# Matmuls grouped by their width, and the first layer's attention in pairs with its division on GpSimd

## The chip, the core and the metric

The kernel runs on one core of a Trainium2 chip. The metric is the device time of one execution in microseconds. A core has engines that run side by side: TensorE (PE: matmuls; PEld: the loads of their stationary operand), VectorE (DVE), ScalarE (ACT), GpSimd (POOL) and SyncE (SP), which here issues nearly all DMAs. An engine runs its own instructions in order; semaphores join the engines.

## What is computed

Two transformer layers on 256 tokens of width 1024 in float32, each followed by a squared-ReLU MLP of width 4096, then a final RMSNorm. The first (even) layer has 8 heads of neighbourhood attention (NA) beside 8 heads of latent attention (MLA); the second (odd) layer has 16 heads of dilated windows in three groups.

```python
def even_mixer(xn, w_in, rpb, ...):
    hcat = xn @ w_in
    out_a = neighbourhood_attention(q, k, v, rpb)          # softmax(q k / 8 + bias) v, 8 heads of 64
    out_b = dense_attention(q, k, v, (64 + 32) ** -0.5)    # 8 heads, q and k of 96, v of 64
    return jnp.concatenate([out_a, out_b], axis=-1) @ w_o

def sq_relu_mlp(xn, w1, w2):
    return jnp.square(jax.nn.relu(xn @ w1)) @ w2

for layer in range(2):
    x = x + (even_mixer if layer == 0 else odd_mixer)(rms_norm(x, norm_mix[layer]), ...)
    x = x + sq_relu_mlp(rms_norm(x, norm_mlp[layer]), mlp_w1[layer], mlp_w2[layer])
return rms_norm(x, norm_final)
```

## The kernel before

**Number format.** A float32 operand is split into a high and a low part (`split`, L200: a CAST on ACT makes `whi`, a subtraction on DVE makes `wlo`), and a product is the sum of three matmuls, high by high, high by low and low by high. `mm3` (L204) issues them as three matmuls of one width. Where the moving operand is the layer's input, its two parts lie side by side (`pair_tile`, L87: 256 tokens high, 256 low), and two matmuls do: a **wide** one of 512 columns, `whi` by both parts, and a **narrow** one of 256 columns, `wlo` by the high part. Both have a 128x128 stationary operand.

**Where wide and narrow matmuls are.** `up` in `mlp` (L390 and L391): 32 steps (16 in each MLP), each with two PSUM banks (f = 0, 1) and 8 k, so 16 wide and 16 narrow in turn. Between two `up` steps stand the 24 matmuls of a `down` step, all 512 wide (`mm3`). In the odd layer `gemm` of `qk_steps` (L905, L906): 24 weights, two banks each, 8 k, in two halves of 4 k; between the halves and the banks stands attention work (`weave`). In the first `up` step of an MLP the wide matmul of k needs the parts of the input that `join` (L298) has just made: DVE adds the layer's output to x (L301), ACT makes the high part (L241), DVE the low part (L242), two k at a time. `hand_over` runs the last steps of the output projection (`out_last`, on PE) and these joins.

**The first layer's attention.** 16 items, 8 of NA and 8 of MLA; an item is a pair of heads (hp) by a half of the tokens (t). An item has three steps. `scores` (L730): on PE 6 matmuls with 64 rows (NA, `two_heads`, L214) or with 96 (MLA); then on DVE two reductions (L748 or L751), on ACT two exponentials (L753), on DVE a reciprocal (L754), on ACT two scalings by it (L756). `turn_probs` (L759): four transposes on PE (L763) and a copy out. `mix` (L767): eight matmuls of 64 columns (L777; float32, so a trace has two records for each of four pairs), and a `split` of the 128x128 result. `attention()` lists the steps item by item; the loop at L818 puts them between the steps of `main` (projections, then the output projection), each of which carries a cost number, in proportion to the cost that has gone by.

**Second layer's attention** has the same three steps; its `mix` (L995) puts two halves of the tokens into two banks, with one `split` each. **The end** (`finish`, L489 to L509): the last 128 tokens are scaled by their norm in two halves, one on DVE and one on ACT, each stored by its engine's own DMA (SP's for DVE).

PE, ACT, DVE and POOL instructions are ordered by a scheduler that keeps dependencies and follows priorities (`tc.high_priority`); weights come through four `raw` buffers, loaded four ahead and split two ahead (L192).

Of the kernel before, what the change touches and what calls it, by code (L numbers as in the profile page):

```python
# [16 lines left out]
F32 = mybir.dt.float32  # L17
# [23 lines left out]
NORM_PRIO = 300  # L41

# [26 lines left out]
def trunk(ctx, tc, a, out):  # L69
# [304 lines left out]
    def mlp(mp, xT, s, invert, tail, make_down, beside=lambda j: None):  # L374
# [4 lines left out]
        def up(j):  # L379
            w = weight()  # L380


            pu = [bank("w") for _ in range(2)]

            ranges = [range(4), range(4, 6), range(6, 8)] if j == 0 else [range(8)]
            for ks in ranges:
                for f in range(2):
                    for k in ks:
                        c = slice(k * 256 + f * P, k * 256 + f * P + P)
                        nc.tensor.matmul(two(pu[f]), w[0][:, c], xT[2][:, k], start=k == 0, stop=False)  # L390
                        nc.tensor.matmul(pu[f][:, 0:T], w[1][:, c], xT[0][:, k, :], start=False, stop=k == KT - 1)  # L391
# [48 lines left out]
    def finish(mp, xT, s):  # L440
# [49 lines left out]
        xg = [scratch([512], "xg") for _ in range(2)]  # L490
        residual(1, HALF[1], accs[3])
        for i, (c0, c1) in enumerate(((0, 512), (512, 768), (768, D))):
# [11 lines left out]
            nc.vector.tensor_tensor(xg[c0 // 512][:, c0 % 512:c0 % 512 + c1 - c0], v, g[:, c0:c1], op=ALU.mult)  # L504
        r = rsqrt(ss[:, 3:4], "x")
        nc.vector.tensor_scalar(xg[0], xg[0], r, None, ALU.mult)
        nc.sync.dma_start(out[P:T, HALF[0]], xg[0])
        nc.scalar.activation(xg[1], xg[1], AF.Copy, scale=r)
        nc.scalar.dma_start(out[P:T, HALF[1]], xg[1])  # L509


    def even(ep):
# [208 lines left out]
        items = [(0, t, hp) for hp in range(4) for t in range(NT)] + [(1, t, hp) for hp in range(4) for t in range(NT)]  # L721
# [8 lines left out]
        def scores(n):  # L730
# [24 lines left out]
            for j in range(2):  # L755
                nc.scalar.activation(pp[:, j], pp[:, j], AF.Copy, scale=rz[:, j:j + 1])  # L756
# [10 lines left out]
        def mix(n):  # L767
            kind, t, hp = items[n]
            pts = turned.pop(n)
# [3 lines left out]
            pvo = bank("acc" if n < 6 else "w")  # L773
            for kk in range(NT):
                for j in range(2):
                    h = 2 * hp + j
                    nc.tensor.matmul(pvo[64 * j:64 * j + 64, 0:P], v[:, kk, h * 64:(h + 1) * 64], pts[:, 2 * j + kk, :],  # L777
                                     start=kk == 0, stop=kk == NT - 1)
            split(*(z[:, hp, tok(t)] for z in mixed[kind]), pvo[:, 0:P])

        def attention():

            out = []
            for n in range(len(items) + 2):
# [3 lines left out]
                if n == 0:  # L788
                    out += [lambda: None] * 2
# [373 lines left out]
```

## Time and profile before

| what | value |
|---|---|
| median of 3 runs (lowest to highest) | 747.52 us (747.17 to 747.56) |
| the profiled execution | 746.66 us |
| its span, first to last instruction | 744.8 us |
| TensorE clock granted, mean | 0.999 |
| PE busy | 737.3 us, 99% of the span |
| DVE, ACT, POOL busy | 539.9, 473.6, 8.3 us |
| first layer, up to the first wide matmul of its MLP | 0 to 113.4 us |

A busy PE says little by itself: a matmul's shown duration covers its way through the array, and neighbours overlap (a wide one shows 397 ns, and the next starts about 230 ns later). So the pace is read from starts: first and last start of a run of like matmuls, over their number. "Who waited for whom" and the chain of work that ended last tell whether PE stood still.

### The profile page before, as it was taken

How to read it: one execution, taken by the hardware profiler on the slowest of the kernel's cores; microseconds unless marked ns; L12 is line 12 of the kernel's file. 1: busy time of each engine (PE TensorE's matmuls, PEld its weight loads, DVE VectorE, ACT ScalarE, POOL GpSimd, SP SyncE). 2: the span in 40 equal slices, each digit the busy share in tenths (PEclk: the TensorE clock that was granted, in tenths of full speed). 3: DMA queues.
4: the chain of work that ended last, by engine and by line, in shares of the span. 5: the costliest groups of instructions: out<-in, count | busy, mean ns of one | idle time of the engine just before them, and what ended most of it. 6: DMA issues, size and time to landing. Idle time of an engine off the chain costs nothing.

```text
span 744.8 us, 12006 instructions
## 1 busy us (share of the span) xinstructions
PE 737.3 (99%) x4539; PEld 634.8 (85%) x4539; DVE 539.9 (72%) x1109; ACT 473.6 (64%) x1027; POOL 8.3 (1%) x20
## 2 busy tenths in 40 slices
PE   9999999999999999999999999999999999999996
PEld 7998998888888887888888888888898888888885
DVE  6778858766666667689968886899558765665664
ACT  7788866554554556468877768687856544554541
POOL 0100000000000001000000000000000000000000
PEclk9999999999999999999999999999999999999999
DMA  9772334565555554645654555455545556555501
GB/s 292 309 272 97 118 113 166 175 222 178 187 201 178 191 196 152 234 159 172 213 209 144 191 175 180 136 194 169 194 148 181 194 191 205 184 177 191 193 13 56
DMA packets 24585, 133.17 MB, mean 179 GB/s; under 512 B 3664, under 2 KB 4688, under 8 KB 10192
## 3 DMA queue, kind: packets, MB, share of 16 engines
q1 hardware_dynamic: 24384, 132.15, 51.4%
q8 instruction: 35, 0.57, 0.3%
q10 hardware_dynamic: 144, 0.26, 0.1%
q14 instruction: 22, 0.18, 0.1%
HBM read 127.16 MB, written 1.05 MB: 172 GB/s over the span
## 4 chain that ended last, share of the span: by engine, by line
PE 97%; issue 1%; ACT 1%; DVE 0%; POOLq 0%; POOL 0%
PE w L390 16%; PE acc L205 13%; PE acc L207 13%; PE acc L206 13%; PE acc L905 12%; PE w L391 8%; PE acc L906 6%; PE acc L553 3%; PE w L214 1%; PE w L991 1%; PE w L205 1%; PE w L207 1%; PE w L763 1%; PE w L206 1%; PE w L971 1%
## 5 line engine op out<-in xcount | busy, mean ns | idle before, releaser
L202 DVE TENSOR_TENSOR wlo<-raw,whi 128x512 fp32r<-128x512 f32 (+2 forms) x471 | 304.6, 680 | 128.7 <-ACT whi L201 128.0
L201 ACT CAST whi<-raw 128x512 fp32r<-128x512 f32 (+2 forms) x471 | 262.4, 615 | 173.4 <-PE w L390 62.4
L390 PE MATMUL w<-pair,whi 128*128 128x512 f32 x512 | 182.2, 397 | 0.0
L391 PE MATMUL w<-pair,wlo 128*128 128x256 f32 x512 | 144.2, 282 | 0.0
L905 PE MATMUL acc<-pair,whi 128*128 128x512 f32 x384 | 139.2, 403 | 0.0
L390 PEld LDWEIGHTS w<-pair,whi 128*128 128x128 f32 x512 | 96.5, 189 | 23.1
L906 PE MATMUL acc<-pair,wlo 128*128 128x256 f32 x384 | 108.1, 282 | 0.0
L205 PE MATMUL acc<-whi,hh 128*128 128x512 f32 x250 | 98.2, 393 | 0.0
L207 PE MATMUL acc<-whi,hl 128*128 128x512 f32 x250 | 97.9, 391 | 0.0
L206 PE MATMUL acc<-wlo,hh 128*128 128x512 f32 x250 | 97.8, 391 | 0.0
L391 PEld LDWEIGHTS w<-pair,wlo 128*128 128x128 f32 x512 | 96.1, 188 | 0.9
L905 PEld LDWEIGHTS acc<-pair,whi 128*128 128x128 f32 x384 | 72.4, 189 | 16.8 <-issue 0.2
L906 PEld LDWEIGHTS acc<-pair,wlo 128*128 128x128 f32 x384 | 72.3, 188 | 0.0
L207 PEld LDWEIGHTS acc<-whi,hl 128*128 128x128 f32 x250 | 47.0, 188 | 9.9
L205 PEld LDWEIGHTS acc<-whi,hh 128*128 128x128 f32 x250 | 47.0, 188 | 9.8
L206 PEld LDWEIGHTS acc<-wlo,hh 128*128 128x128 f32 x250 | 47.0, 188 | 8.9
L394 ACT COPY side<-w 128x256 f32<-128x256 f32 x64 | 23.6, 369 | 22.1 <-PE w L391 22.1
L205 PE MATMUL acc<-whi,pair 128*128 128x512 f32 x80 | 32.4, 405 | 0.0
L207 PE MATMUL acc<-whi,pair 128*128 128x512 f32 x80 | 31.5, 394 | 0.0
L206 PE MATMUL acc<-wlo,pair 128*128 128x512 f32 x80 | 31.2, 390 | 0.0
L395 DVE TENSOR_TENSOR u<-w,side 128x256 f32<-128x256 f32 x64 | 26.9, 420 | 3.7 <-ACT side L394 3.0
L201 ACT CAST hh<-hsq 128x512 fp32r<-128x512 f32 x32 | 19.9, 622 | 10.1 <-DVE hsq L397 10.1
(221 smaller groups left out, 1102.9 us busy)
## 6 DMA issues: line engine op xcount, KB each, us to landing
raw<-in_w SPq DMA_DIRECT2D x64, 1024.0 KB, 4.9
raw<-in_w_oqk SPq DMA_DIRECT2D x24, 1024.0 KB, 5.2
raw<-in_w_ov SPq DMA_DIRECT2D x12, 1024.0 KB, 4.9
raw<-in_w_qk SPq DMA_DIRECT2D x4, 1024.0 KB, 8.9
raw<-in_w_oe SPq DMA_DIRECT2D x4, 1024.0 KB, 5.0
sw<-qk SPq DMA_DIRECT2D x64, 64.0 KB, 2.1
raw<-in_w_oo SPq DMA_DIRECT2D x4, 1024.0 KB, 5.0
bias<-in_rpb SPq DMA_DIRECT2D x8, 256.0 KB, 3.9
```

Of the source, the lines that this page charges most:

```text
L201: a = nc.scalar.copy(hi, src).ins
L202: return a, (eng or nc.vector).tensor_tensor(lo, src, hi.bitcast(F32), op=ALU.subtract).ins
L205: nc.tensor.matmul(o, sh, mh, start=first, stop=False)
L206: nc.tensor.matmul(o, sh, ml, start=False, stop=False)
L207: nc.tensor.matmul(o, sl, mh, start=False, stop=last)
L390: nc.tensor.matmul(two(pu[f]), w[0][:, c], xT[2][:, k], start=k == 0, stop=False)
L391: nc.tensor.matmul(pu[f][:, 0:T], w[1][:, c], xT[0][:, k, :], start=False, stop=k == KT - 1)
L394: nc.scalar.copy(side[:, f], pu[f][:, T:2 * T])
L395: nc.vector.tensor_tensor(u[:, f], pu[f][:, 0:T], side[:, f], op=ALU.add)
L553: nc.tensor.matmul(o[:, 0:n], xs[i], (w[1], w[1], w[2])[i], start=(k, i) == (0, 0), stop=(k, i) == (KT - 1, 2))
L905: nc.tensor.matmul(two(pq), wh[:, ws], xp[:, k], start=k == 0, stop=False)
L906: nc.tensor.matmul(pq[:, 0:T], wl[:, ws], xh[:, k, :], start=False, stop=k == KT - 1)
```

## The change

- `up` and the odd layer's `qk_steps` issue a bank's wide matmuls in a run and then the narrow ones in a run. In `up` all 16 wide ones of both banks come first; in `qk_steps` 6 wide ones make the first half, 2 wide and 8 narrow the second.
- The first layer's attention goes by pairs of items (the two token halves of one hp): at a set cost (`PAIRS_AT`) the scores of both, then the mix of the pair before, in one bank with one `split` of 128x256; the two `turn_probs` come 2.5 and 3.4 later.
- The scaling by the reciprocal is on POOL in place of ACT.
- The latent projections' transposes come two steps after their matmuls throughout; the two `turn_c` steps stand later.
- The odd layer's `mix` uses one bank and one `split`; at the end ACT scales and stores 256 columns, DVE 768.

The diff, cut to its core:

```diff
+
+PAIRS_AT = (5.0, 9.4, 13.8, 18.2, 23.6, 27.6, 31.5, 35.4)
+PAIRS_END = 39.6
...
             ranges = [range(4), range(4, 6), range(6, 8)] if j == 0 else [range(8)]
+            cut_of = lambda k, f: slice(k * 256 + f * P, k * 256 + f * P + P)
             for ks in ranges:
                 for f in range(2):
                     for k in ks:
-                        c = slice(k * 256 + f * P, k * 256 + f * P + P)
-                        nc.tensor.matmul(two(pu[f]), w[0][:, c], xT[2][:, k], start=k == 0, stop=False)
-                        nc.tensor.matmul(pu[f][:, 0:T], w[1][:, c], xT[0][:, k, :], start=False, stop=k == KT - 1)
+                        nc.tensor.matmul(two(pu[f]), w[0][:, cut_of(k, f)], xT[2][:, k], start=k == 0, stop=False)
+            for f in range(2):
+                for k in range(KT):
+                    nc.tensor.matmul(pu[f][:, 0:T], w[1][:, cut_of(k, f)], xT[0][:, k, :], start=False, stop=k == KT - 1)
...
-        nc.vector.tensor_scalar(xg[0], xg[0], r, None, ALU.mult)
-        nc.sync.dma_start(out[P:T, HALF[0]], xg[0])
-        nc.scalar.activation(xg[1], xg[1], AF.Copy, scale=r)
-        nc.scalar.dma_start(out[P:T, HALF[1]], xg[1])
+        c = slice(768, D)
+        nc.scalar.activation(xg[:, c], xg[:, c], AF.Copy, scale=r)
+        nc.scalar.dma_start(out[P:T, c], xg[:, c])
+        c = slice(0, 768)
+        nc.vector.tensor_scalar(xg[:, c], xg[:, c], r, None, ALU.mult)
+        nc.sync.dma_start(out[P:T, c], xg[:, c])
 
...
-                nc.scalar.activation(pp[:, j], pp[:, j], AF.Copy, scale=rz[:, j:j + 1])
+                nc.gpsimd.tensor_scalar(pp[:, j], pp[:, j], rz[:, j:j + 1], None, ALU.mult)
...
+        def mix(p, tag):
+
+            kind, _, hp = items[2 * p]
             if mixed[kind] is None:
                 mixed[kind] = quarter_pair("ob")
             v = (vna, vml)[kind]
-            pvo = bank("acc" if n < 6 else "w")
-            for kk in range(NT):
-                for j in range(2):
-                    h = 2 * hp + j
-                    nc.tensor.matmul(pvo[64 * j:64 * j + 64, 0:P], v[:, kk, h * 64:(h + 1) * 64], pts[:, 2 * j + kk, :],
-                                     start=kk == 0, stop=kk == NT - 1)
-            split(*(z[:, hp, tok(t)] for z in mixed[kind]), pvo[:, 0:P])
+            pvo = bank(tag)
+            for n in (2 * p, 2 * p + 1):
+                pts, tk = turned.pop(n), tok(items[n][1])
+                for kk in range(NT):
+                    for j in range(2):
+                        h = 2 * hp + j
+                        nc.tensor.matmul(pvo[64 * j:64 * j + 64, tk], v[:, kk, h * 64:(h + 1) * 64], pts[:, 2 * j + kk, :],
+                                         start=kk == 0, stop=kk == NT - 1)
+            with tc.high_priority(NORM_PRIO):
+                split(*(z[:, hp, :] for z in mixed[kind]), pvo[:, 0:T])
 
         def attention():
 
+
             out = []
-            for n in range(len(items) + 2):
-                for fn, m in ((scores, n), (turn_probs, n - 1), (mix, n - 2)):
-                    if 0 <= m < len(items):
...
-                if n == 0:
-                    out += [lambda: None] * 2
-            return out
+            for p, at in enumerate(PAIRS_AT):
+                tag = "acc" if p < 5 else "w"
+
+                def start(p=p, tag=tag):
+                    for n in (2 * p, 2 * p + 1):
+                        scores(n)
+                    if p:
+                        mix(p - 1, tag)
+                out.append((at, start))
+                out += [(at + d, lambda n=2 * p + k: turn_probs(n)) for k, d in enumerate((2.5, 3.4))]
+            return out + [(PAIRS_END, lambda: mix(len(PAIRS_AT) - 1, "w"))]
...
 
 
         accs, wo = [], {}
         main = [(1.31, f) for c in range(1, 4) for f in qk_steps(c)]
-        main.insert(1, (0, turn_c[1]))
+        main[3:3] = [(0, turn_c[1])]
+        main[2:2] = [(0, turn_c[0])]
         i = lambda t, h: 2 * t + h
-        for h in range(2):
-            main += [(.65, kg[i(0, h)]), (.98, ug[i(0, h)]), (.43, kt[i(0, h)]), (.65, kg[i(1, h)]), (.43, ut[i(0, h)]),
-                     (.98, ug[i(1, h)]), (.43, kt[i(1, h)]), (.43, ut[i(1, h)])]
+
+        made = [f for h in range(2) for t in range(NT) for f in ((.65, kg[i(t, h)], kt[i(t, h)]), (.98, ug[i(t, h)], ut[i(t, h)]))]
+        for n in range(len(made) + 2):
+            if n < len(made):
+                main.append(made[n][:2])
+            if n >= 2:
+                main.append((.43, made[n - 2][2]))
         main += [(0, lambda: accs.extend(open_accs()))]
         main += [(1.3, f) for k in range(6) for f in out_steps(accs, mixed, wo, k)]
-        side = attention()
-        at = -5
-        total = sum(c for c, _ in main) + at
-        done = 0
+        side, at = attention(), 0
         for c, f in main:
             f()
             at += c
-            while done < len(side) and done * total < at * len(side):
-                side[done]()
-                done += 1
+            while side and side[0][0] <= at:
+                side.pop(0)[1]()
+        assert not side
...
-                    ws = slice((f * KT + k) * P, (f * KT + k + 1) * P)
-                    nc.tensor.matmul(two(pq), wh[:, ws], xp[:, k], start=k == 0, stop=False)
-                    nc.tensor.matmul(pq[:, 0:T], wl[:, ws], xh[:, k, :], start=False, stop=k == KT - 1)
+
+                cut_of = lambda k: slice((f * KT + k) * P, (f * KT + k + 1) * P)
+                for k in (range(0, 6), range(6, KT))[half]:
+                    nc.tensor.matmul(two(pq), wh[:, cut_of(k)], xp[:, k], start=k == 0, stop=False)
+                if half == 1:
+                    for k in range(KT):
+                        nc.tensor.matmul(pq[:, 0:T], wl[:, cut_of(k)], xh[:, k, :], start=False, stop=k == KT - 1)
...
             def mix(out_tag):
-                pvo = [bank(out_tag) for _ in range(NT)]
+                pvo = bank(out_tag)
...
                             cs = slice(64 * j, 64 * j + 64)
-                            nc.tensor.matmul(pvo[i][cs, 0:P], v0[:, kk, cs], turned[i, j][:, kk, :], start=kk == 0, stop=False)
...
                             cs = slice(64 * j, 64 * j + 64)
-                            nc.tensor.matmul(pvo[i][cs, qs], v12[:, 2 * i + c, cs], turned[i, j][:, 2, qs], start=False, stop=c == 1)
...
+                            nc.tensor.matmul(pvo[cs, i * P + 64 * c:i * P + 64 * c + 64], v12[:, 2 * i + c, cs], turned[i, j][:, 2, qs], start=False, stop=c == 1)
                 with tc.high_priority(NORM_PRIO):
-                    for i in range(NT):
-                        split(*(z[:, u % 4, tok(i)] for z in mixed[u // 4]), pvo[i][:, 0:P])
```

On PE, in the middle of an MLP (`up`, `pair` is the layer's input, `whi` and `wlo` the weight's parts), before:

```order
L390 MATMUL w<-pair,whi 128x512
L391 MATMUL w<-pair,wlo 128x256
L390 MATMUL w<-pair,whi 128x512
L391 MATMUL w<-pair,wlo 128x256
L206 MATMUL acc<-wlo,hh 128x512
L207 MATMUL acc<-whi,hl 128x512
```

and now:

```order
L210 MATMUL acc<-whi,hl 128x512
L394 MATMUL w<-pair,whi 128x512 x16
L397 MATMUL w<-pair,wlo 128x256 x16
L208 MATMUL acc<-whi,hh 128x512
L209 MATMUL acc<-wlo,hh 128x512
```

The same 32 matmuls stand between the same neighbours, with one change of width inside in place of 31.

On PE, in the first layer's NA part (`qk_h`, `qk_l`: an hp's queries and keys; `pts`: turned probabilities; `ch`: the latent input; `pp`: probabilities), before:

```order
L777 MATMUL acc<-pts,vna 64x128 x4
L214 MATMUL w<-qk_h 128x256 x2
L214 MATMUL w<-qk_l,qk_h 128x256 x2
L214 MATMUL w<-qk_h,qk_l 128x256 x2
L205 MATMUL acc<-whi,ch 128x512
L206 MATMUL acc<-wlo,ch 128x512
L207 MATMUL acc<-whi,cl 128x512
L763 MATMUL w<-ident,pp 128x128 x4
```

and now:

```order
L210 MATMUL acc<-pair,wlo 128x256
L217 MATMUL w<-qk_h 128x256 x2
L217 MATMUL w<-qk_l,qk_h 128x256 x2
L217 MATMUL w<-qk_h,qk_l 128x256 x2
L217 MATMUL w<-qk_h 128x256 x2
L217 MATMUL w<-qk_l,qk_h 128x256 x2
L217 MATMUL w<-qk_h,qk_l 128x256 x2
L787 MATMUL acc<-pts,vna 64x128 x8
L208 MATMUL acc<-pair,whi 128x256
```

Two items' scores and the mix of the two items before stand in one place. The eighth mix and one NA pair are an exception: the last mix stands in two halves, and the fourth pair's scores and mix alternate. After the first pair's scores come 24 projection matmuls, then the first item's transposes, 12 more, and the second item's.

On POOL, the whole of the first layer after its norms, before:

```order
L565 TENSOR_TENSOR rstd<-ss,mhalf 128x2 x2
L710 COPY ktok<-kpe 128x4x32 x4
L839 MEMSET k_0_3254 128x1024
```

and now:

```order
L573 TENSOR_TENSOR rstd<-ss,mhalf 128x2 x2
L764 TENSOR_SCALAR pp<-pp,rz 128x256 x12
L718 COPY ktok<-kpe 128x4x32 x2
L764 TENSOR_SCALAR pp<-pp,rz 128x256 x4
L718 COPY ktok<-kpe 128x4x32 x2
L764 TENSOR_SCALAR pp<-pp,rz 128x256 x16
L856 MEMSET k_0_3230 128x1024
```

32 scalings of 256 columns have come to POOL's queue, around the four copies that the MLA keys need.

## Rows read from the trace of the kernel before

**Rows 1.** The page, chain that ended last, shares of the span by engine.

```profile
PE 97%; issue 1%; ACT 1%; DVE 0%; POOLq 0%; POOL 0%
```

**Rows 2.** Groups by line and shape, PE: count | busy us, mean ns | idle.

```profile
L390 PE MATMUL w<-pair,whi 128*128 128x512 f32 x512 | 182.2, 397 | 0.0
L905 PE MATMUL acc<-pair,whi 128*128 128x512 f32 x384 | 139.2, 403 | 0.0
```

**Rows 3.** Timeline, PE: start us, us, instruction; pairs, then a wide run.

```profile
149.84 0.40 PE L390 MATMUL w<-pair,whi 128*128 128x512 f32 x1
...
153.02 0.40 PE L390 MATMUL w<-pair,whi 128*128 128x512 f32 x1
...
153.37 0.39 PE L205 MATMUL acc<-whi,hh 128*128 128x512 f32 x1
...
154.53 0.40 PE L207 MATMUL acc<-whi,hl 128*128 128x512 f32 x1
...
158.84 0.39 PE L390 MATMUL w<-pair,whi 128*128 128x512 f32 x1
```

**Rows 4.** Timeline, PE: two runs of narrow matmuls that follow wide ones.

```profile
26.07 0.28 PE L205 MATMUL w<-pair,whi 128*128 128x256 f32 x1
...
30.05 0.28 PE L207 MATMUL w<-pair,wlo 128*128 128x256 f32 x1
...
735.01 0.28 PE L205 MATMUL w<-whi,hh 128*128 128x256 f32 x1
...
737.89 0.28 PE L205 MATMUL w<-whi,hh 128*128 128x256 f32 x1
```

**Rows 5.** Timeline, PE: an item's scores between projection matmuls.

```profile
38.21 0.28 PE L207 MATMUL acc<-pair,wlo 128*128 128x256 f32 x1
38.41 0.38 PE L214 MATMUL w<-qk_h 64*128 64x256 f32 x2
...
38.96 0.39 PE L205 MATMUL acc<-pair,whi 128*128 128x256 f32 x1
39.19 0.28 PE L206 MATMUL acc<-pair,whi 128*128 128x256 f32 x1
```

**Rows 6.** Chain in order of time: start, us; scores and mixes of both sizes.

```profile
38.48 0.55 PE w L214 x6
...
47.14 0.59 PE acc L777 x8
...
420.21 0.91 PE w L214 x12
421.12 1.02 PE w L971 x16
```

**Rows 7.** Timeline at the first hand-over: PE's first wide matmul; DVE's last join.

```profile
113.42 0.40 PE L390 MATMUL w<-pair,whi 128*128 128x512 f32 x1
...
115.09 1.68 DVE L242 SCALAR_TENSOR_TENSOR pair<-gx,pair 128x256 fp32r<-128x256 f32 x4
```

**Rows 8.** Timeline, ACT: the first item's two scalings.

```profile
41.43 0.91 ACT L756 ACTIVATE pp<-pp,rz 128x256 f32<-128x256 f32 x2
```

**Rows 9.** Groups by line and shape, POOL: the four copies of 128 columns.

```profile
L710 POOL COPY ktok<-kpe 128x128 f32<-128x128 f32 x4 | 1.2, 292 | 34.2 <-DVE qk_l L202 25.5 <-PE acc L777 8.6
```

**Rows 10.** Timeline: two powers on POOL, and DVE beside the second.

```profile
27.42 0.70 POOL L565 TENSOR_TENSOR rstd<-ss,mhalf 128x2 f32<-128x2 f32 x1 [1.43 <-DVE ss L563]
31.88 1.06 POOL L565 TENSOR_TENSOR rstd<-ss,mhalf 128x2 f32<-128x2 f32 x1 [3.76 <-DVE ss L563]
...
31.70 0.69 DVE L202 TENSOR_TENSOR wlo<-raw,whi 128x512 fp32r<-128x512 f32 x1
```

**Rows 11.** Busy us of PE, PEld, DVE, ACT, POOL (x instructions), clock, DMA share.

```profile
60.00:80.00 20.00, 20.00 (x166) 17.07 (x163) 18.33 (x61) 18.43 (x53) 0.59 (x2) 1.00 0.20 67
```

**Rows 12.** Timeline, the last scalings on DVE and on ACT.

```profile
740.60 0.49 DVE L506 TENSOR_SCALAR xg<-xg,rstd 128x512 f32<-128x512 f32 x1 [0.45 <-POOL rstd L232]
...
740.60 0.72 ACT L508 ACTIVATE xg<-xg,rstd 128x512 f32<-128x512 f32 x1 [2.86 <-POOL rstd L232]
```

More of the change, by code (lines that the diff above doesn't have):

```diff
@@ L489, in finish @@
         ss = work.tile([P, 4], F32, tag="ssf", name="ss")
-        xg = [scratch([512], "xg") for _ in range(2)]
+        xg = mp.tile([P, D], F32, name="xg")
         residual(1, HALF[1], accs[3])
@@ L720, in even @@
         mixed = [quarter_pair("oa"), None]
-        items = [(0, t, hp) for hp in range(4) for t in range(NT)] + [(1, t, hp) for hp in range(4) for t in range(NT)]
+        items = [(kind, t, hp) for kind in range(2) for hp in range(4) for t in range(NT)]
         biases, probs, turned = {}, {}, {}
@@ L765, in turn_probs @@
             nc.any.tensor_copy(out=turned[n], in_=pt.rearrange("p (b n) -> p b n", b=4))
-        def mix(n):
-            kind, t, hp = items[n]
-            pts = turned.pop(n)
+        def mix(p, tag):
+            kind, _, hp = items[2 * p]
             if mixed[kind] is None:
@@ L902, in gemm @@
                 (wh, wl), pq, q32 = hold["w"], hold["p"], hold["q"]
-                for k in range(4 * half, 4 * half + 4):
-                    ws = slice((f * KT + k) * P, (f * KT + k + 1) * P)
-                    nc.tensor.matmul(two(pq), wh[:, ws], xp[:, k], start=k == 0, stop=False)
-                    nc.tensor.matmul(pq[:, 0:T], wl[:, ws], xh[:, k, :], start=False, stop=k == KT - 1)
+                cut_of = lambda k: slice((f * KT + k) * P, (f * KT + k + 1) * P)
[4 more added lines that the diff above has]
+                        nc.tensor.matmul(pq[:, 0:T], wl[:, cut_of(k)], xh[:, k, :], start=False, stop=k == KT - 1)
                 if half == 1:
@@ L1001, in mix @@
                             cs = slice(64 * j, 64 * j + 64)
-                            nc.tensor.matmul(pvo[i][cs, 0:P], v0[:, kk, cs], turned[i, j][:, kk, :], start=kk == 0, stop=False)
+                            nc.tensor.matmul(pvo[cs, tok(i)], v0[:, kk, cs], turned[i, j][:, kk, :], start=kk == 0, stop=False)
                     for c in range(2):
@@ L1006, in mix @@
                             cs = slice(64 * j, 64 * j + 64)
-                            nc.tensor.matmul(pvo[i][cs, qs], v12[:, 2 * i + c, cs], turned[i, j][:, 2, qs], start=False, stop=c == 1)
+                            nc.tensor.matmul(pvo[cs, i * P + 64 * c:i * P + 64 * c + 64], v12[:, 2 * i + c, cs], turned[i, j][:, 2, qs], start=False, stop=c == 1)
                 with tc.high_priority(NORM_PRIO):
-                    for i in range(NT):
-                        split(*(z[:, u % 4, tok(i)] for z in mixed[u // 4]), pvo[i][:, 0:P])
+                    split(*(z[:, u % 4, :] for z in mixed[u // 4]), pvo[:, 0:T])
             return scores, [lambda v=(i, j): turn(*v) for i in range(NT) for j in range(2)], mix
```

4 lines of the change are left out of this document (1 added, 3 removed).

## The prediction

> **What bounds the kernel now.** I read the chain of work that ended last first: PE carries 97% of it [rows 1], so the time is the sum of PE's steps from start to start, and another engine counts only where PE comes to wait for it. Next the groups by line: 512 and 384 wide matmuls stand in wide-narrow pairs, 896 pairs in all, and PE sat idle 0.0 us before them [rows 2]: what can shrink there is the pace, not a wait. So the timeline comes last, read by starts. In the mixed stretch nine pairs take 153.02 - 149.84 = 3.18 us, 0.3533 a pair [rows 3]. In a run of wide matmuls alone, 24 steps from 153.37 to 158.84 take 5.47, 0.2279 each; the first five, just behind a narrow one, take 1.16, 0.232 each [rows 3]. A run of narrow ones behind wide ones steps by 3.98/35 = 0.1137 in one place and 2.88/24 = 0.1200 in another [rows 4]. In runs a pair would so cost 0.342 to 0.352 in place of 0.353. That is the change's first source, small each time but taken 896 times.
>
> **The sum, part by part.** I work against the profiled execution, 746.66 us (span 744.8), 0.86 under the median of 747.52.
>
> *Widths in the MLPs.* Each of 32 steps holds 16 pairs. Its wide run follows wide matmuls, so it goes at 0.2279; for the narrow run I take 0.1168, the middle of two rows that differ and of which I can't say which is nearer (one has the same operands, the other stands in the same MLP). A pair saves 0.3533 - 0.2279 - 0.1168 = 0.0086, a step 0.138, all 4.4 us. Ends: 16 x 0.0117 x 32 = 6.0 and 16 x 0.0054 x 32 = 2.8.
>
> *Widths in the odd layer.* 48 groups of 8 pairs, mostly entered from a narrow matmul or from attention work, so I take 0.232 for the wide ones: 8 x (0.3533 - 0.232 - 0.1168) = 0.036, x 48 = 1.7 us. Ends: 8 x 0.0117 x 48 = 4.5, and 8 x 0.0013 x 48 = 0.5. Together **-6.1** (-3.3 to -10.5).
>
> *Fewer visits to other tile shapes.* Scores (64 rows) and mixes (64 columns) cost PE more than their own work: the step into scores is 38.41 - 38.21 = 0.20 where narrow ones step by 0.114, and the first projection matmul behind them takes 39.19 - 38.96 = 0.23 [rows 5]; that is 0.09 and 0.11 of turning. Inside, 6 score matmuls cost 0.55 and 12 cost 0.91, so joining two visits saves 2 x 0.55 - 0.91 = 0.19; 8 of the mix cost 0.59, and the 16 of the odd layer's scores of the same shape 1.02, so joining saves 0.16 [rows 6]. With the turning, 0.39 for joined scores and 0.36 for joined mixes. NA's scores join four times (1.6), mixes eight times, of which the last stands in two halves and one is cut up by scores: 6 to 8 x 0.36 = 2.2 to 2.9. MLA's 96-row scores enter four times in place of eight; I put that at 0.1 each, as the turning above, 0.4. Sum **-4.5** (-3.6 to -5.2). The scores that now touch a mix gain about what the ones that touched it before did.
>
> *The hand-over.* In an MLP's first step the wide matmuls of k 4 come behind 8 wide ones, at 113.42 + 8 x 0.228 = 115.24; before, behind 8 pairs, at 116.25. DVE's last four low parts run from 115.09, 0.42 each [rows 7]: k 4 is ready at 115.51, k 5 at 115.93. PE waits 0.27 for the first and 0.19 for the second; k 6 and 7 (116.35, 116.77) are then in time. Two hand-overs: **+0.9** (0.3 to 1.6). DVE's queue keeps its order there.
>
> *The division on POOL and the new times.* ACT loses 32 scalings, two in 0.91 [rows 8]; PE didn't wait for ACT, so that alone is worth nothing. POOL shows no such scaling. From below: its copy of half the size takes 0.29 [rows 9]; from above, 1.06, its longest small operation [rows 10]. I take 0.5, by the copy, which is nearest: an operation on columns of SBUF. Two in turn are 1.0, about ACT's 0.91. In the trace the first item's scalings end 42.34 - 38.96 = 3.4 after its scores have left PE [rows 5, 8]. Now its transposes stand behind the second item's scores (0.35) and 24 matmuls x 0.114 = 2.7 plus 0.2 of turning: 3.3. So the first pair is about 0.2 late; the later ones have a mix ahead too (0.9) and are on time in the first item, but the second item, whose exponentials and scalings queue behind the first's, has about 4.5 against a chain of 3.4 + 1.1 + 0.1. I book 0.1 to 0.2 a pair, **+1.0**.
>
> POOL also gets in DVE's way. A power of 128x2 takes 0.70 alone and 1.06 when it starts at 31.88 inside a DVE subtraction of two SBUF operands that ends at 32.39 [rows 10]; the four copies, beside DVE work that reads PSUM at their start or end, stay at 0.29 [rows 9]. So POOL can wait some 0.36 for such a subtraction. Whether DVE is held in turn no row shows: between 0 and a scaling's 0.5 each time. DVE is busy 18.33 of 20 us in the fullest stretch [rows 11], and 32 delays of 0.25, the middle, would be 8 us of DVE time over 65, mostly in its gaps. With some scalings 0.36 later than booked above I add **+0.5**. The Trainium skill, page "SBUF — State Buffer", section "Who interferes with whom", has a rule against this edit: DVE and GpSimd share one pair of SBUF ports, a DVE operation with two SBUF inputs contends with a GpSimd one that reads SBUF, and the loser blocks for the whole instruction; POOL's wait agrees with it, and DVE's, which it also foretells, would put this term at rival (4)'s price. Both POOL terms: +1.5 (0 to 6).
>
> *The rest.* One bank and one split a mix take work off DVE and ACT, hidden under PE. At the end ACT's last scaling halves from 0.72, DVE's grows from 0.49 [rows 12]; the later of two stores starts about 0.1 sooner and is larger: **-0.1** (-0.4 to 0.3).
>
> Sum: -6.1 - 4.5 + 0.9 + 1.5 - 0.1 = -8.3, 738.4 for the profiled execution, with 0.86 a median of **739.2 us**.
>
> **Rivals.** (1) *The width gain isn't there*: the 0.353 of a pair belongs to these operands and not to the alternation. For it: no row has wide `pair` matmuls in a run, and a narrow run has been seen at 0.120. Against: narrow ones with the same `pair` operand ran at 0.1137. Only visits, waits and end remain: -4.5 + 0.9 + 1.5 - 0.1 = -2.2, **745.3**. (2) *A run goes at the clock*: columns stream with no extra. The granted clock is 0.999 of its upper level, 2.4 GHz, so 768 columns are 0.320; 896 x 0.033 = 29.9 in place of 6.1, **715**. Against it stand both runs of [rows 3, 4], above 0.213 and 0.107. The Trainium skill, page "TensorE: Matmul & The Clock Gate", section "Back-to-back issue gap", gives N / 2.4 + 2.5 ns, 0.325 for a pair in runs, an estimate that would save 25 us; the trace's runs are slower than that. (3) *Slower: POOL becomes the bound in the first layer.* If a scaling costs 1.06 [rows 10], a pair's four take 4.2; the second item is ready 1.1 x 2 later still, some 2.4 late before its transposes, PE stands, and nothing makes it up: 8 x 2.4 = 19 in place of 1.0, **757**. It turns the whole to a loss from about 1.2 late a pair, a scaling of some 0.75 us. For it: POOL's small operations are slow in the trace; against: its copy. (4) *DVE falls behind from the shared operands*: all 32 delays of 0.5 hit a full DVE, a third of 16 us reaches PE: about +4.5 in place of 0.5, **743**.
>
> **How the numbers follow.** The forecast 0.72, (1) 0.12, (2) 0.04, (3) 0.06, (4) 0.06. The forecast's own ends: widths -3.3 to -10.5, visits -3.6 to -5.2, waits; they don't all fall one way, so about 734 to 743. The range takes in (4) and most of (1): 733.0 to 745.0. What this kernel's measurement can tell from no change is 0.2%, 1.5 us: 746.0 to 749.0. The forecast lies below that but for 0.01, (1) for 0.09 of its 0.12, (2) and (4) wholly, (3) above it for 0.05: faster 0.90, same 0.05, slower 0.05.
>
> **What would show it.** In the trace after: the starts in `up`, 16 wide steps near 0.228 and 16 narrow ones at 0.114 to 0.120; the stretch from one `up` to the next 0.14 shorter than before; the first wide matmul of the MLP some 3 us earlier than 113.4; a gap of about 0.3 before k 4 in the first `up`; POOL's scalings at 0.5 each, and DVE's subtractions at 0.68 or longer beside them. I am wrong if the narrow run steps by over 0.122 or the wide one by over 0.235, if POOL's scaling takes over 0.75, or if PE shows gaps of over 1 us before the transposes.

## The result, and the profile after

The changed kernel takes **748.51 us** (median, 748.13 to 749.48); the kernel before, on the same chip in the same rounds, 747.17. The ratio is 1.0018, interval 1.0012 to 1.0025: slower by 0.18%, within the 0.2% that this kernel's measurement can tell from no change, and far above the forecast range. The profiled span is 746.6 us, 1.8 longer than before.

The chain that ended last shows something new at once. PE carried 97% of it [rows 1]; now, on the page, with POOL's groups below it:

```profile
PE 88%; DVE 3%; POOL 3%; issue 2%; ACT 2%; DMA 1%; SPq 1%; POOLq 0%; DVEq 0%; ACTq 0%
...
L764 POOL TENSOR_SCALAR pp<-pp,rz 128x256 f32<-128x256 f32 x32 | 33.8, 1073 | 42.2 <-DVE rz L762 35.5
```

The windows (columns as in [rows 11]) say where: PE was busy for all of 60 to 80 us before; now it has holes in the whole stretch of attention.

```profile
40.00:60.00 20.00, 17.25 (x162) 15.06 (x161) 13.61 (x42) 10.32 (x34) 9.29 (x9) 1.00 0.70 235
60.00:80.00 20.00, 18.56 (x135) 14.86 (x134) 15.23 (x51) 14.95 (x41) 9.29 (x12) 1.00 0.22 77
80.00:100.00 20.00, 18.57 (x170) 17.31 (x169) 14.93 (x43) 13.87 (x40) 11.06 (x11) 1.00 0.44 151
```

ACT and DVE are less busy there than before and PE waits all the same, so the cause is not an engine that is full but one that is late. The waits from 36 to 119 us (engine, line, releaser: us in all, times, longest) name it, and the chain in order of time shows one case:

```profile
POOL pp L764 <- DVE rz L762: 35.5, 7, 8.4
...
PEld w L771 <- POOL pp L764: 9.3, 14, 1.2
...
PE w L771 <- POOL pp L764: 5.9, 11, 1.0
```

```profile
41.03 0.14 DVE rz L762
41.17 0.09 issue
41.26 4.96 POOL pp L764 x4
46.22 0.04 issue
46.27 0.44 PE w L771 x2
```

L771 is the transposes, L764 the division. POOL divides the four head blocks of a pair one behind the other, 4.96 us, and PE's last transposes of the pair start 0.05 after the last of them. Yet POOL itself idled for 35.5 us, waiting for the sums: it has room, but it answers late.

By stages, read from PE's starts: from its first step to the first wide matmul of the first MLP, that MLP, the odd layer (its first projection to the last steps of its output projection) and the second MLP: 112.23, 171.19, 255.17, 180.54 us before; 118.09, 169.86, 253.59, 179.26 after. The two hand-overs left out between them are alike, 18.2 us together in both. So +5.9 in the first layer, and -1.3, -1.6 and -1.3 where only widths changed (and the mixes of the odd layer). The gain is there, and is given back.

In an MLP step the runs look like this (start, us, instruction, count):

```profile
153.53 3.89 PE L394 MATMUL w<-pair,whi 128*128 128x512 f32 x16
157.26 1.99 PE L397 MATMUL w<-pair,wlo 128*128 128x256 f32 x16
159.09 0.39 PE L208 MATMUL acc<-whi,hh 128*128 128x512 f32 x1
...
164.54 1.79 PE L394 MATMUL w<-pair,whi 128*128 128x512 f32 x7
```

From start to start the 16 wide ones take 3.73, 0.233 each, and the narrow ones 1.83, 0.114 each; the stretch from one `up` to the next is 11.01; before, by 16 pairs and the run behind them [rows 3], it was 16 x 0.3533 + 5.47 = 11.12.

**An account of the first layer.** For each kernel below I added PE's steps, start to start, between the first scores and the first MLP's first wide matmul. The account holds what goes beyond the usual step of a projection, transpose or other matmul (0.114 for 256 columns, 0.227 for 512, and so on): scores and mixes with the turning into and out of them, waits (a step over 0.2 longer than usual), and all other lengthening. The usual steps sum to 55.7 us in every one of them. The rows of e7 and e9 each hold some 1.7 us that a stretch at the lower clock adds (under e7), most of it in mixes and projections.

| kernel | scores (visits) | mixes (visits) | other | waits |
|---|---|---|---|---|
| before | 5.6 (8) | 12.9 (17) | 0.9 | 0 |
| changed | 4.8 (6) | 10.4 (11) | 1.8 | 8.2 |
| e1: changed, division on ACT | 5.0 (6) | 10.8 (12) | 1.5 | 1.7 |
| e2: before, division on POOL | 5.6 (8) | 12.3 (16) | 1.9 | 4.7 |
| e4: pairs alone, on ACT | 5.0 (6) | 10.8 (12) | 1.6 | 1.7 |
| e7: POOL, transposes later | 5.1 (5) | 10.7 (10) | 1.2 | 8.1 |
| e8: one head on each | 5.1 (6) | 10.3 (11) | 2.0 | 2.7 |
| e9: ACT, transposes later | 5.2 (5) | 10.6 (10) | 1.6 | 1.9 |
| e11: POOL, behind next scores | 4.2 (4) | 11.2 (12) | 0.6 | 3.8 |
| e12: e11, one head on each | 4.3 (4) | 11.6 (13) | 0.6 | 3.8 |

### The profile page after: what moved, and what is told of

Same layout as the page of the kernel before. It is cut to its first block, busy times and chain, and to the rows that moved or that the text cites. A ratio compares the mean times of both kernels' runs of the same rounds, so it can differ in the third digit from the quotient of the medians.

```text
span 746.6 us, 12005 instructions
## 1 busy us (share of the span) xinstructions
PE 732.4 (98%) x4539; PEld 628.2 (84%) x4539; DVE 535.9 (72%) x1087; ACT 460.2 (62%) x985; POOL 42.5 (6%) x52
## 4 chain that ended last, share of the span: by engine, by line
PE 88%; DVE 3%; POOL 3%; issue 2%; ACT 2%; DMA 1%; SPq 1%; POOLq 0%; DVEq 0%; ACTq 0%
PE w L394 16%; PE acc L208 12%; PE acc L210 12%; PE acc L209 12%; PE acc L923 11%; PE w L397 8%; PE acc L926 5%; POOL pp L764 3%; PE acc L561 2%; PE w L1011 1%; PE w L217 1%; PE w L991 1%; PE w L209 1%; PE w L208 1%; PE w L210 1%
## 5 line engine op out<-in xcount | busy, mean ns | idle before, releaser
L394 PE MATMUL w<-pair,whi 128*128 128x512 f32 x512 | 125.1, 395 | 0.0
L394 PEld LDWEIGHTS w<-pair,whi 128*128 128x128 f32 x512 | 95.0, 187 | 23.1 <-DVE pair L245 1.0
L923 PE MATMUL acc<-pair,whi 128*128 128x512 f32 x384 | 101.6, 401 | 0.0
L923 PEld LDWEIGHTS acc<-pair,whi 128*128 128x128 f32 x384 | 67.7, 188 | 12.4 <-issue 0.2
L397 PEld LDWEIGHTS w<-pair,wlo 128*128 128x128 f32 x512 | 63.5, 188 | 3.0
L397 PE MATMUL w<-pair,wlo 128*128 128x256 f32 x512 | 64.0, 277 | 0.0
L926 PEld LDWEIGHTS acc<-pair,wlo 128*128 128x128 f32 x384 | 51.2, 188 | 4.4
L926 PE MATMUL acc<-pair,wlo 128*128 128x256 f32 x384 | 51.9, 277 | 0.0
L764 POOL TENSOR_SCALAR pp<-pp,rz 128x256 f32<-128x256 f32 x32 | 33.8, 1073 | 42.2 <-DVE rz L762 35.5
```

What stands on the lines that cost most here:

```text
L394: nc.tensor.matmul(two(pu[f]), w[0][:, cut_of(k, f)], xT[2][:, k], start=k == 0, stop=False)
L397: nc.tensor.matmul(pu[f][:, 0:T], w[1][:, cut_of(k, f)], xT[0][:, k, :], start=False, stop=k == KT - 1)
L764: nc.gpsimd.tensor_scalar(pp[:, j], pp[:, j], rz[:, j:j + 1], None, ALU.mult)
L923: nc.tensor.matmul(two(pq), wh[:, cut_of(k)], xp[:, k], start=k == 0, stop=False)
L926: nc.tensor.matmul(pq[:, 0:T], wl[:, cut_of(k)], xh[:, k, :], start=False, stop=k == KT - 1)
```

## The experiments

**Theory T**: PE waits for the four divisions in a row on POOL, and that is the whole of what the forecast lacks. **Rival R**: the set times are too tight for the chain, whoever divides. **Rival (4)** of the forecast: DVE is held by POOL. The first four runs take the change apart (before measured 746.92 beside them).

*e1, the division back on ACT.*

```diff
-                nc.gpsimd.tensor_scalar(pp[:, j], pp[:, j], rz[:, j:j + 1], None, ALU.mult)
+                nc.scalar.activation(pp[:, j], pp[:, j], AF.Copy, scale=rz[:, j:j + 1])
```

> The changed kernel with one thing undone: the first layer's probabilities are again multiplied by the reciprocal of their sum on ACT, not on POOL. Theory T (the four POOL scalings of a pair, 0.92 us each and up to 1.85 beside DVE, are late before the pair's transposes, and this is the whole of what the forecast lacks): the time falls by 9 to 10 us to about 738 to 739; PE's idle time before the transposes of the attention goes under 1 us in all, the first wide matmul of the first MLP comes near 110 instead of 119.3. Rival R (the set times are too tight for the chain of maximum, exponential, sum, reciprocal and division, whoever divides): above 744, and PE still idles 0.5 us and more before the transposes of most of the eight pairs.

Measured 742.23 us, ratio 0.9937 (0.9925 to 0.9950): 6.3 less than the changed kernel (6.0 when each is set against the kernel before beside it), not 9 to 10, and the MLP's first wide matmul comes at 113.68, not near 110. T names the cause rightly and says too much. The waits before the transposes shrink to the first line here, but ACT brings one of its own, of 1.0 us (under e4):

```profile
PEld w L771 <- ACT pp L764: 1.6, 5, 0.7
...
PEld acc L208 <- ACT kh L204: 1.1, 1, 1.1
...
PE acc L208 <- DVE r L547: 0.8, 1, 0.8
```

*e2, the kernel before with the division on POOL* (e1's edit the other way, at L756).

> The kernel before with one thing done: the same division moved from ACT to POOL, in the order and at the places of before (one item at a time, two scalings each). Theory T: POOL's scaling takes 0.92 alone and 1.2 and more beside DVE here too, an item's two take 1.9 to 2.5 instead of ACT's 0.9, so an item is 1.0 to 1.6 later, but an item's transposes stand farther behind its scores than in pairs: 1 to 5 us slower than before, 748 to 752. Rival R (POOL is not what costs; the set times are): within 1 us of before.

Measured 752.23, ratio 1.0073 (1.0060 to 1.0085), 5.3 slower: a little over T's upper end. Without pairs and set times POOL costs nearly as much, so R's condition isn't needed. The waits:

```profile
PEld w L763 <- POOL pp L756: 5.6, 9, 1.2
...
PE w L763 <- POOL pp L756: 3.5, 7, 1.0
```

*e3, the kernel before with the widths alone.*

```diff
-                        nc.tensor.matmul(pu[f][:, 0:T], w[1][:, c], xT[0][:, k, :], start=False, stop=k == KT - 1)
...
+            for f in range(2):
+                for k in range(KT):
+                    nc.tensor.matmul(pu[f][:, 0:T], w[1][:, cut_of(k, f)], xT[0][:, k, :], start=False, stop=k == KT - 1)
...
```

> The kernel before with one thing done: runs of one width in the MLPs and in the odd layer's projections. Theory T: by the stages of the changed kernel the MLPs are 1.33 and 1.28 shorter, the odd layer 1.6, together 4.2 us: 743.0, between 742 and 744. If the odd layer's 1.6 came from its joined mixes instead, 744.6. The forecast on record had -6.1, 741.1.

Measured 742.40, ratio 0.9937 (0.9923 to 0.9950): 4.5 us gained. The odd layer's stage is 253.49 where it was 255.17, so its gain is the widths' and not the joined mixes'.

*e4, the pairs, set times, joined mixes and tail alone*: the changed kernel with e1's edit and the old wide-narrow order.

> The changed kernel with two things undone: the division back on ACT, and the matmuls again in wide-narrow pairs. What is left is the attention by pairs at set times, the joined mixes and the tail. Theory T: the forecast's term for fewer visits, -4.5, holds and nothing is late: 742.5 to 743.5. Rival R (the set times are too tight): 747 or more.

Measured 746.56, ratio 0.9994 (0.9986 to 1.0003). Neither: nothing gained, nothing lost. By the account the visits to scores and mixes save 2.7 us, 0.7 come back in other steps and 1.7 as waits. The larger wait, in the timeline:

```profile
69.89 0.50 ACT L759 ACTIVATE pp<-sn,mn 128x256 f32<-128x256 f32 x1
...
70.38 0.36 ACT L693 COPY qtok<-acc 128x256 f32<-128x256 f32 x1
...
71.05 0.35 DVE L545 TENSOR_TENSOR r<-acc,sinr 128x64 f32<-128x64 f32 x2
...
71.54 0.41 PE L208 MATMUL acc<-whi,ch 128*128 128x384 f32 x1 [0.77 <-DVE r L545]
```

PE waits for DVE, which reads out a PSUM bank; DVE waited for a copy on ACT, which stood behind an exponential. It is ACT's queue, and with the division on POOL this wait isn't there. The parts add up: -4.5 (e3) and -0.4 (e4) make -4.9, where e1, which has both, measured -4.7; the rest of the changed kernel's +1.3 is the division, +6.0.

The next four ask how POOL costs it, and one thing on the widths (before measured 746.96 beside them).

*e5, POOL busy with nobody waiting*: e1, and behind it

```diff
+            for j in range(2):
+                nc.gpsimd.tensor_scalar(idle_pp, idle_pp, rz[:, j:j + 1], None, ALU.mult)
```

> The changed kernel with the division back on ACT (742.2 us), and POOL doing the same two scalings an item beside it, on a tile of its own that nobody reads. This takes the wait for POOL away and leaves POOL's use of SBUF beside DVE. Theory T (what costs is that PE waits for POOL's result): 742.0 to 743.2, and no wait for POOL on PE. Rival (4) of the forecast (DVE is held by the shared operands and PE waits for DVE): 744 to 748; DVE's subtractions of 128x512 are longer than 0.68 in both cases.

Measured 742.98, ratio 0.9943 (0.9932 to 0.9955). As T has it; 0.75 over e1, with intervals that overlap. No wait for POOL stands on PE (its weight load waits once, 0.3, for a key copy that now queues behind POOL's scalings).

*e7, later transposes*: the division on POOL, and

```diff
-                out += [(at + d, lambda n=2 * p + k: turn_probs(n)) for k, d in enumerate((2.5, 3.4))]
+                out += [(at + d, lambda n=2 * p + k: turn_probs(n)) for k, d in enumerate((3.6, 4.0))]
```

> The changed kernel, division on POOL, with one line altered: a pair's transposes stand at 3.6 and 4.0 of the plan's units behind the pair's start instead of 2.5 and 3.4, so that 12 more projection matmuls (2.8 us) stand between scores and transposes and the transposes of a pair mostly stand together. Theory T (the loss is waiting for a chain that is too long for its place, not POOL's work as such): PE's 8 us of waits before the transposes fall under 2; 748.5 - 6.5, with about one more for fewer visits 740 to 742, as fast as the division on ACT or faster. Rival R (POOL can't keep up, so the wait only moves on to the mixes): 745 or more.

Measured 749.17 (746.5 to 751.1), ratio 1.0025 (1.0014 to 1.0037). A miss. My 2.8 us was wrong to begin with: the 12 matmuls moved are narrow, 1.4 us, and they move the first item alone. POOL's four start at 41.88 and end at 46.83, and PE stands before the third and the fourth head:

```profile
41.88 4.95 POOL L764 TENSOR_SCALAR pp<-pp,rz 128x256 f32<-128x256 f32 x4 [9.02 <-DVE rz L762]
```

```profile
44.12 0.60 PE L771 MATMUL w<-ident,pp 128*128 128x128 f32 x4
...
45.68 0.44 PE L771 MATMUL w<-ident,pp 128*128 128x128 f32 x2 [0.96 <-POOL pp L764]
...
46.89 0.33 PE L771 MATMUL w<-ident,pp 128*128 128x128 f32 x1 [0.77 <-POOL pp L764]
```

Elsewhere the transposes, now close to the next scores, keep those waiting for a bank: among the waits,

```profile
PE w L771 <- POOL pp L764: 5.2, 7, 1.8
PE w L217 <- ACT pts L773: 0.9, 1, 0.9
```

Part of this run's time is TensorE's clock. In the profiled execution the granted clock is at the lower of its two levels, 1.2 GHz, for 3.41 us, shortly after PE had stood 1.84 and 0.46 us before transposes (last row: a window, columns as in [rows 11]):

```profile
84.25 0.44 PE L771 MATMUL w<-ident,pp 128*128 128x128 f32 x2 [1.84 <-POOL pp L764]
85.16 0.44 PE L771 MATMUL w<-ident,pp 128*128 128x128 f32 x2 [0.46 <-POOL pp L764]
...
86.71:90.12 3.41, 3.41 (x24) 2.85 (x23) 2.38 (x12) 2.08 (x8) 0.00 (x0) 0.50 0.15 58
```

The 16 records of a pair's mix take 1.91 there from start to start, 1.03 in the same run at 76.69; the whole stretch costs some 1.7 us. The twelve times follow the mean granted clock, from 746.50 twice at 0.998 to 750.98 and 751.09 at 0.992; the changed kernel's twenty lie at 0.997 to 0.999, and its trace is at 2.4 GHz up to the tail. So the median hides a gain: where the clock holds, the later transposes are some 2 us faster than the changed kernel, though far from 740 to 742. The run doesn't tell lag from pace; e11 was made for that.

*e8, one head on ACT and one on POOL.*

```diff
+                if j == 0:
+                    nc.scalar.activation(pp[:, j], pp[:, j], AF.Copy, scale=rz[:, j:j + 1])
+                else:
+                    nc.gpsimd.tensor_scalar(pp[:, j], pp[:, j], rz[:, j:j + 1], None, ALU.mult)
```

> The changed kernel with the division of an item's first head on ACT and of its second on POOL, side by side; places as in the changed kernel. POOL's chain of a pair is then two scalings, 1.9 to 2.5 us, where it was 3.6 to 5.1. Theory T: the second item of a pair no longer queues behind the first, and the waits before the transposes fall from 8 us to between 1 and 3: 742 to 744.5. If a single scaling's length beside DVE (1.2 to 1.85) is what costs: 745 to 747.

Measured 743.20, ratio 0.9952 (0.9940 to 0.9963). Half the chain takes away 5.3 of the 6.3 us, though the scalings themselves are as long as ever (0.92, with four of 16 between 1.2 and 1.8): it is the queue of four that costs, not the length of one.

*e10, flat operands*: e1, and

```diff
-                        nc.tensor.matmul(two(pu[f]), w[0][:, cut_of(k, f)], xT[2][:, k], start=k == 0, stop=False)
+                        nc.tensor.matmul(pu[f], w[0][:, cut_of(k, f)], xT[2][:, k].rearrange("p f n -> p (f n)"), start=k == 0, stop=False)
...
```

> The changed kernel with the division back on ACT (742.2 us), and the wide matmuls of both kinds of layer written with flat operands of 512 columns instead of two times 256; same addresses, same order. It asks why the wide runs step by 0.2335 where the run that the forecast took its 0.2279 from is flat. If the written shape is the cause: 0.2279 again, 896 x 0.0055 = 4.9 us less, 737.3. If it isn't: 742.2, and the steps stay at 0.2335.

Measured 742.25, ratio 0.9939 (0.9924 to 0.9953), and 16 steps take 3.74, 0.234 each: the written shape isn't it.

```profile
158.21 3.89 PE L394 MATMUL w<-pair,whi 128*128 128x512 f32 x16
161.95 1.99 PE L397 MATMUL w<-pair,wlo 128*128 128x256 f32 x16
```

The last four (before 747.04, and 746.83 beside e12).

*e9, later transposes with the division on ACT*: e1's edit and e7's.

> The changed kernel with the division on ACT and a pair's transposes at 3.6 and 4.0 of the plan's units instead of 2.5 and 3.4. It asks where the forecast's 4.5 us for fewer visits stayed: with the division on ACT at the old places PE changes its tile shape 86 times in the stretch of attention (85 before the change), because the transposes are laid singly between the projections; here 59 times. If the changes of shape are what counts: 27 fewer at 0.09 to 0.11, less the turning they share, and some 1 us of waits before the transposes gone: 739.0 to 740.5. If the waits only move (four transposes of an item at once, one bank later free): 742 or more.

Measured 742.25, ratio 0.9931 (0.9919 to 0.9944), by the median as e1. But the profiled execution is at 1.2 GHz for 3.41 us, after a wait that moved to the scores, for a bank:

```profile
62.71 0.38 PE L217 MATMUL w<-qk_h 64*128 64x256 f32 x1 [1.28 <-ACT pts L773]
...
64.54:67.95 3.41, 3.41 (x20) 2.98 (x16) 1.10 (x6) 2.52 (x9) 0.00 (x0) 0.50 0.49 207
```

Its mean clock is 0.995, and so is that of two other runs of the five. The remaining two, at 0.997 and 0.999, took 740.58 and 741.38, below all five of e1 (742.02 to 742.52). So the median doesn't answer the question: where the clock holds, the later transposes look worth about 1 us, by two runs only, and whether fewer visits or shorter waits bring it stays open. It is not the transposes' shape: where PE doesn't wait, in e1 the step into a run of them is 0.004 longer than usual, and at its end the last transpose's step is 0.08 shorter and the next projection's 0.09 longer, so transposes of 128 by 128 between projections aren't a visit to another shape.

*e11, the division on POOL and the transposes behind the next pair's scores.*

```diff
+PAIRS_AT = (5.0, 9.2, 13.4, 17.6, 22.4, 26.0, 29.6, 33.2)
+TURNS, MIX = (5.0, 5.6), 6.4
...
+                out += [(at, lambda n=2 * p + k: scores(n)) for k in range(2)]
+                out += [(at + d, lambda n=2 * p + k: turn_probs(n)) for k, d in enumerate(TURNS)]
+                out.append((at + MIX, lambda p=p, tag=tag: mix(p, tag)))
...
```

> The changed kernel with the division on POOL, the transposes of a pair put behind the scores of the next pair (5.0 and 5.6 of the plan's units behind the pair's start), the mix of the pair right behind them (6.4), and the pairs' starts a little closer (5.0, 9.2, 13.4, 17.6, 22.4, 26.0, 29.6, 33.2) so that all fits. PE then has some 5 to 7 us of other work between a pair's scores and its transposes where the changed kernel has 3 to 5, against POOL's chain that ended up to 7 behind the scores. Theory T (the wait is for the length of POOL's chain): PE's waits for POOL fall from 8 us to under 2.5, the time to 741 to 743.5. Rival (POOL's pace, not its lag, is the bound; or the longer lives of the tiles make new waits): 746 or more, with the same waits at other places.

Measured 742.70, ratio 0.9944 (0.9931 to 0.9958). As T has it: POOL does the same 32 scalings (0.92 to 1.43), the first pair's four again in 4.95, and they are done at 46.90, before PE's first transposes of that pair start:

```profile
41.95 4.95 POOL L764 TENSOR_SCALAR pp<-pp,rz 128x256 f32<-128x256 f32 x4 [8.41 <-DVE rz L762]
```

```profile
47.82 0.63 PE L771 MATMUL w<-ident,pp 128*128 128x128 f32 x4 [1.19 <-DVE mn L756]
```

This shows that lag and not pace was the cost. The waits of the run are now mostly for copies and banks; the last row here is the weight load for that same start, and POOL had ended 0.9 before it:

```profile
PEld acc L787 <- ACT pts L773: 2.0, 1, 2.0
...
PE acc L787 <- ACT pts L773: 1.7, 1, 1.7
...
PEld w L771 <- POOL pp L764: 1.4, 1, 1.4
```

*e6, prices on POOL*: e1, with four operations that nobody reads beside it.

```diff
+                    nc.gpsimd.tensor_scalar(idle_pp[:, 0:P], idle_pp[:, 0:P], rz[:, v:v + 1], None, ALU.mult)
...
+                    nc.gpsimd.tensor_scalar(idle_pp, idle_pp, 0.5, None, ALU.mult)
...
+                    nc.gpsimd.tensor_copy(idle_pp[:, 0:P], idle_pp[:, P:T])
...
+                    nc.gpsimd.tensor_copy(idle_pp[:, 0:P].rearrange("p (h n) -> p h n", h=4), kpe[:, 0, :].unsqueeze(1).broadcast_to([P, 4, 32]))
```

> The changed kernel with the division on ACT, and four small POOL operations beside it that nobody reads, two of each an item: the scaling by a column on 128 columns; a scaling by a constant on 256; a copy of 128 columns; the copy with a repeated operand that the forecast took its price from. If POOL's price is by the column and the kind of operation: the scaling of 128 takes about half of 0.92, 0.45 to 0.5, and the copies 0.29. If most of 0.92 is a fixed price of a scaling with a column operand: 128 columns take 0.7 or more, and the constant on 256 less than 0.92. The shortest of each counts, since DVE lengthens the others. Its time says nothing (between 742 and 745).

By line, ns least/median/most (743.8 us in its one run):

```profile
L770 POOL TENSOR_SCALAR idle_pp<-idle_pp,rz x8: 603/744/1195, 42.0 to 97.1; 128x128 f32<-128x128 f32 x8
```

```profile
L772 POOL TENSOR_SCALAR idle_pp<-idle_pp x8: 847/890/1289, 44.5 to 98.7; 128x256 f32<-128x256 f32 x8
```

```profile
L774 POOL COPY idle_pp<-idle_pp x8: 289/294/1043, 46.7 to 100.0; 128x128 f32<-128x128 f32 x8
```

The copy with a repeated operand takes 0.293. Neither expectation holds for the scaling: 128 columns are 0.60, 256 are 0.92 (the other runs), so 0.32 per 128 columns (2.5 ns a column) and 0.28 fixed. At equal size it costs twice the copy.

*e12, e11's places with e8's halves.*

> The layout of the run before (transposes behind the next pair's scores, mix right behind them), with the first head's division on ACT and the second's on POOL. It asks whether the two halves of the cause add up: a shorter chain, and more work before it is needed. By the accounts of the runs with either alone (742.7 and 743.2), which each kept 2.7 to 3.8 us of waits, and with each scores visit whole (4.2 us instead of 4.9 to 5.1): waits under 2, 740 to 741.5. If the waits that were left are not for the division (banks, the copies of the transposes, ACT's queue): 742 or more.

Measured 743.78, ratio 0.9967 (0.9955 to 0.9979). The two cures don't add; the waits stay at 3.8. The largest stands at L677, the transposes of the latent keys:

```profile
76.72 0.50 PE L677 MATMUL w<-ident,ktok 128*96 128x128 f32 x3 [2.19 <-POOL pp L767]
```

```profile
75.89 0.69 DVE L205 TENSOR_TENSOR kl<-w,kh 96x512 fp32r<-96x512 f32 x1
```

The profile puts it down to POOL's scalings, but these transposes read from POOL only the key copies, done at 67.84; just before them, at 76.58, DVE ends the low part of the keys, which empties a bank. So I read it as a wait for a bank and not for the division; no run tests that.

So e3, e1, e9, e10 and e11, at medians of 742.2 to 742.7, beat the kernel before by 0.6% and the changed one by 0.8%; by the medians none is told from the plainest, e3.

## Why the prediction was wrong, point by point

- **The step that failed: the price of the division on POOL, and with it the wait for a pair.** I took 0.5 us "by the copy, which is nearest: an operation on columns of SBUF". It is 0.92 alone and up to 1.85 beside DVE. Size and kind were both passed over: the copy [rows 9] has half the columns, and at equal size half the price (e6). With 0.5 I had 0.2 late a pair; the text itself put the turn to a loss at 0.75. Forecast +1.0, measured 8.2 us of waits, of which 1.7 stand with the division on ACT too (e1). The other end of my own bounds, 1.06 [rows 10], was the nearer row: the mean of the 32 is 1.07. Two of the signs that the prediction named for being wrong came: a scaling over 0.75, and gaps over 1 us before the transposes (1.1 by the account's steps).
- **Rival (3) is what happened**, at a chance of 0.06. Its 19 us was too much: it counted 2.4 us late for every pair against a PE that never stands. But when PE stands for the first item, the second gets that time as well; the first pair stood 1.1 and 0.7, and the eight lost 1.0 each in the mean.
- **Contention (+0.5)**: borne out in size (e5's 0.75 over e1, not told from nothing). Whether DVE is held, which no row showed, is settled: in e1 its low-part subtractions take at most 0.693 us, in the changed kernel up to 0.893, some 1 us in all; in e5, where POOL works and nobody waits for it, up to 0.891. The first row is e1's, the second the changed kernel's, the third POOL there (ns least/median/most):

```profile
L205 DVE TENSOR_TENSOR wlo<-raw,whi x35: 419/681/693, 42.1 to 110.8; 128x512 fp32r<-128x512 f32 x27, 128x256 fp32r<-128x256 f32 x4, 128x384 fp32r<-128x384 f32 x4
```

```profile
L205 DVE TENSOR_TENSOR wlo<-raw,whi x35: 408/678/893, 41.4 to 116.2; 128x512 fp32r<-128x512 f32 x27, 128x256 fp32r<-128x256 f32 x4, 128x384 fp32r<-128x384 f32 x4
```

```profile
L764 POOL TENSOR_SCALAR pp<-pp,rz x32: 913/926/1850, 41.3 to 109.4; 128x256 f32<-128x256 f32 x32
```

  So rival (4)'s 0.5 a time was too much as well. The rule of the Trainium skill that I cited, in "SBUF — State Buffer", section "Who interferes with whom", that a DVE operation with two SBUF inputs and a GpSimd one that reads SBUF contend, agrees with these rows in both directions; POOL loses more by it, some 5 us over the 32. That the loser is held for a whole instruction, as I put it, they don't show: DVE's longest grew by 0.2 beside scalings of 0.92 and more.
- **Fewer visits (-4.5)**: -3.2 in the changed kernel (before the table's rounding), less 0.9 of other lengthening, so -2.3. The mixes came as worked out (-2.5, forecast 2.2 to 2.9). The scores gave 0.7, not 1.6: I counted four joined visits, but the fourth pair's scores are cut in three by the mix of the pair before, six visits and not four; with four (e11) it is 1.4. Nothing shows MLA's 0.4.
- **Widths (-6.1) and hand-over (+0.9)**: together -5.2, measured -4.5 (e3), within the bounds given, in part by luck: the gain in the MLPs was too large and the loss at the hand-over too, and the two errors offset each other. The odd layer is right (1.6 for 1.7). In the MLPs a wide step is 0.233, not the 0.228 of the other operands' run, and a narrow one 0.114, not 0.117: 16 x (0.3533 - 0.2331 - 0.1144) = 0.093 a step, 3.0 in all where I had 4.4 (by the stages 2.6, with the first steps in). The hand-over cost nothing to speak of: DVE's four joins began 1.5 us behind the first wide matmul, not 1.7, and the first run steps by 4.00 / 17 = 0.235 (answers to [rows 7]):

```profile
119.28 4.17 PE L394 MATMUL w<-pair,whi 128*128 128x512 f32 x17
123.28 1.93 PE L397 MATMUL w<-pair,wlo 128*128 128x256 f32 x15
```

```profile
120.75 1.67 DVE L245 SCALAR_TENSOR_TENSOR pair<-gx,pair 128x256 fp32r<-128x256 f32 x4
```

- **"PE didn't wait for ACT, so that alone is worth nothing"**: true of the kernel before, not of the pairs. There ACT's queue makes a wait of 1.0 us (e4) that the division on POOL takes away.
- **Tail (-0.1)**: from the last matmul's start to the end of the span 6.5 us, before 6.4; no gain.
- **Rivals (1) and (2)** fall: the runs are faster than pairs, and nowhere near 715.

The sum, as it was: -4.2 in the MLPs and the odd layer, -2.3 visits, +8.2 waits, +0.1 at the end: +1.8, the difference of the spans. Of the 10.1 us between this and the forecast's -8.3, the waits with contention are 6.7, the visits 2.2, widths and hand-over 1.0 and the end 0.2. All of it fell on one side, which "they don't all fall one way" had excluded.

## What to carry to other kernels

Moving a small operation to an idle engine costs its latency on the chain it stands in, times the number that queue there; price it by a row of the same kind and size, and where there is none and a dearer one decides the sign, give the dearer one its weight. An engine that idles most of a stretch can still be what the others wait for; more work between its start and its reader (e11), or half of it on another engine (e8), cures that, and not both are needed. When pieces are joined to save visits, count the visits in the order as built: a neighbour may cut them apart again.

## What the runs showed of the hardware

- POOL's multiplication by a column of scalars costs 0.28 us and 2.5 ns a column (128 columns 0.603 at least, e6; 256 columns 0.92 in the other runs), with a constant 0.85 for 256; ACT does the same 256 columns in some 0.46 [rows 8]. The Trainium skill, page "GPSIMD Engine Reference", section "Engine selection", calls operations with one input on POOL roughly line-rate; these rows, twice ACT's time, don't agree.
- A run of wide matmuls keeps 0.233 a step with these operands and 0.227 with the down projections'; how the operands are written isn't the reason (e10). The reason stays open.
- TensorE's granted clock can fall inside the program: in the traces of e7 and e9 it is at 1.2 GHz for 3.41 us, after PE had stood up to 1.84 and 1.28 us at a time. It isn't every wait that does it: in the changed kernel PE stood 8.2 us in all, up to 1.0 at a time in the profile's count, and its clock stayed at 2.4 GHz there.
